# Weight stores queued behind later loads, more pieces kept from the first block, and one branch around two loops

## The chip, the cores and the metric

The kernel runs on one core of a Trainium2 chip. The core has five engines that run their own instruction streams: TensorE (PE, matrix products, with its weight loads as PEld), VectorE (DVE), ScalarE (ACT), GpSimd (POOL) and SyncE (SP), which here issues almost all DMAs. The streams wait for each other by semaphores. A DMA is issued by one instruction and runs on the core's 16 DMA engines. The metric is the device time of one execution in microseconds (us), the median of several.

## The reference

One decoder block of width 1024 over 2048 tokens, in float32. Cut to its steps:

```
h  = rmsnorm(x, g1);  p = h @ w_in            # q, k, v, r, gate ranks, u, two gates
a  = chunked gated linear attention(q, k, v)  # then per-head norm, times silu(r)
b  = multi-scale causal pooling(u)            # four windows, a map per group
x1 = x + (sig(gg) * (a @ w_a) + sig(gp) * (b @ w_b)) @ w_out
h2 = rmsnorm(x1, g2)
group = top 1 of 4 by softmax(h2 @ w_rg);  2 of the 8 experts of that group
y  = x1 + sum over the two experts of weight * SwiGLU(h2)
out = rmsnorm(y, gf)
```

Each of the 32 experts has a hidden width of 256.

## The kernel before

The tokens are handled in four blocks of 512. For each block `block` projects the inputs, runs the attention in chunks and the pooling branch, forms the gates and merges the two branches (`merge`, products on L757), multiplies by the output weights (`out_mm`, L774), adds the input, normalizes (`out_norm` calls `normed`), turns the result with transposing DMAs (`turn`, L261), and computes the router's logits (`logits`, L796). A block's logits are computed among the products of the next block. After the four blocks come 16 pairs of experts: up and gate products on L1297, down products on L1322 and L1334, the last norm in `finish`, and a scattered store of rows on L1284. At the end `overflow` has two loops that run only if an expert got more rows than its fixed capacity: the first redoes the surplus tiles, the second the last norm. Here both run zero times.

Most products are done in three passes of half-precision parts, so each weight piece (128×1024 float32, 512 KB) has to be split into a high and a low half. `stage` loads the piece (DMA on L161), `halves` converts it (ScalarE L177 for the high half, VectorE L178 for the low one), and the two halves are stored once to a scratch tensor in memory, `wkeep` (DMA on L181), from which later blocks load them with one DMA of the same size (L170). `KEEP` gives for each kind of weight the block from which on its pieces are stored; a piece not stored yet is loaded raw and converted again in the next block. The kinds are, in order: q, k and u; v and r; the two gates; the output weights (8 pieces); the attention branch (4 pieces); the pool branch, which is first folded with the pooling map (L725). Raw and converted pieces share one ring of `NW` = 13 buffers named `w`.

All these loads, stores and the transposing DMAs are issued by SyncE in one order. A DMA whose data isn't ready makes SyncE stand, and what is behind it stands too. The order on each engine is laid down when the program is built, by a scheduler which follows the code's order and the readiness of operands; `issue_after` ties an instruction's place to another's.

Of the kernel before, what the change touches and what calls it, by code (L numbers as in the profile page):

```python
# [16 lines left out]
D = 1024  # L17
KT = 8
# [18 lines left out]
class Mixer:  # L37
# [10 lines left out]
    def pools(self):  # L48
# [14 lines left out]

        self.C, self.kept = tc.dram_tile([16 + 40 + 24, 128, 2, 1024], F16, name="wkeep"), {}
# [24 lines left out]
    def consts2(self):  # L89
# [22 lines left out]
        self.g2q = self.cx.tile([128, D], F32, name="g2q")  # L112
        V.tensor_scalar(self.g2q, self.g2, float(D) ** 0.5, None, op0=OP.mult)
# [45 lines left out]
    def stage(self, mat, i):  # L159
        f = self.wp.tile([128, 1024], F32, name="w", bufs=self.NW)  # L160
        self.nc.sync.dma_start(f, self.A[mat][i])  # L161
        return f

    def weight(self, mat, i, f=None, c=0):

        nc = self.nc
        if (mat, i) not in self.kept:
            return self.halves(f or self.stage(mat, i), (mat, i))
        w = self.wp.tile([128, 2, 1024], F16, name="w", bufs=self.NW)
        nc.sync.dma_start(w[:, :, c:], self.C[self.kept[mat, i]][:, :, c:])  # L170
        return w

    def halves(self, f, key, c=0):
# [19 lines left out]
    KEEP = (1, 1, 0, 1, 1, 0)  # L193
# [10 lines left out]
    NW, NET, NBT = 13, 19, 13  # L204
# [11 lines left out]
    def normed(self, x, g, store=None, quick=False, new=None):  # L216

        nc = self.nc
        if quick:
# [11 lines left out]
            for y, n in zip(ys, q):  # L231
                nc.vector.scalar_tensor_tensor(y, x[:, n], r[:, 0:1], self.g2q[:, n], op0=OP.mult, op1=OP.mult)
# [569 lines left out]
    def block(self, b, tail):  # L802

        last = b + 1 == self.NB
        self.blk = b
        self.hT, self.L7, self.L7c = self.hTn, self.sevens(self.Hn, self.HSn), self.sevens_c(self.Hn, self.HSn)
# [56 lines left out]
        if last:  # L863
            self.xo = {t: self.x_load(b, t) for t in range(TT)}
# [206 lines left out]
    def spill(self):  # L1071
# [31 lines left out]
        V.tensor_scalar(none[:, 0:1], none[:, 0:1], 0.5, None, op0=OP.is_lt)  # L1103
        for _, _, l, _ in self.tab:
# [26 lines left out]
    def moe(self):  # L1131
# [18 lines left out]
        with tc.manual_schedule(engines={getattr(E, e) for e in self.MANUAL}) if self.MANUAL else ExitStack():  # L1150
            for P in range(self.NP + 1):
                for c in (self.PLAN if P else self.PLAN.replace("U0 A0 U1 A1", "V0 V1 W0 A0 W1 A1")).split():
# [186 lines left out]
    def finish(self, s, i):  # L1339

        nc = self.nc
        x, o, _, l, nl = s["X"][i]
        y, r = self.rstd(x)
# [7 lines left out]
        nc.vector.tensor_tensor(y, x, y, op=OP.mult)  # L1351
        t = self.scatter(y, o).ins
# [21 lines left out]
    def overflow(self):  # L1374
# [7 lines left out]
        with tc.For_i(0, n):  # L1382
            T = lambda name, sh, dt=F32: mp.tile([128] + sh, dt, name="o" + name)
            le = T("le", [32])
            V.tensor_scalar(le, self.ct, self.it, None, op0=OP.is_le)
            e = T("e", [1])
            V.tensor_reduce(e, le, axis=AX.X, op=OP.add)
            ei = T("ei", [1], I32)
            V.tensor_copy(ei, e)
            V.tensor_scalar(le, self.i32, e, None, op0=OP.is_equal)  # L1390
            st = T("st", [32])
            V.tensor_tensor(st, self.ct, self.nt, op=OP.subtract)
            V.tensor_tensor(st, st, le, op=OP.mult)
            base = T("base", [1])
            V.tensor_reduce(base, st, axis=AX.X, op=OP.add)
            V.tensor_tensor(base, self.it, base, op=OP.subtract)
            V.tensor_tensor(st, self.capE, le, op=OP.mult)
            cap = T("capt", [1])
            V.tensor_reduce(cap, st, axis=AX.X, op=OP.add)
            V.scalar_tensor_tensor(base, base, 128.0, cap, op0=OP.mult, op1=OP.add)  # L1400
            rel, oth = T("rel", [nt * 2]), T("oth", [nt * 2])
            V.tensor_scalar(oth, self.ex.rearrange("p t k -> p (t k)"), e, OOB, op0=OP.not_equal, op1=OP.mult)
            V.tensor_scalar(rel, self.rk.rearrange("p t k -> p (t k)"), base, None, op0=OP.subtract)
            V.tensor_tensor(rel, rel, oth, op=OP.add)
            io = T("io", [128])
            nc.gpsimd.iota(io, pattern=[[1, 128]], base=0, channel_multiplier=0, allow_small_or_imprecise_dtypes=True)
            pt = self.aux()
            for c in range(2 * nt):
                a = mp.tile([128, 128], F32, name="oA", bufs=1)
                V.tensor_scalar(a, io, rel[:, c:c + 1], None, op0=OP.is_equal)  # L1410
                nc.tensor.matmul(pt[:, 0:2], a, self.fld[:, c // 2, c % 2], start=c == 0, stop=c == 2 * nt - 1)
            tb = T("tb", [2, 1])
            V.tensor_copy(tb, pt[:, 0:2, None])
            ii, w, _, _ = self.columns(tb, "o", mp)
            er = nc.values_load(ei[0:1, 0:1], engines=[mybir.EngineType.SP], min_val=0, max_val=NE - 1,
                                skip_runtime_bounds_check_because="a count of at most 31")
            W = [[self.load(self.A["we"][bass.ds(er, 1), :, c:c + PW].rearrange("o p c -> p (o c)"), i == 2)
                  for c in range(i * 2048, (i + 1) * 2048, PW)] for i in range(3)]
# [114 lines left out]
```

## Time and profile before

| | |
|---|---|
| runs of the kernel, us | 1673.47, 1674.84, 1676.40 (median 1674.84) |
| profiled execution, us | 1676.06, its span 1674.3 |
| mean granted TensorE clock | 0.960 |
| busy in the span, us | PE 1530.3 (91%), DVE 1074.3 (64%), ACT 686.0 (41%), POOL 607.7 (36%) |
| moved by DMA | 294.03 MB read from memory, 75.50 MB written |

The span is the time from the first to the last instruction of the profiled execution, and all positions in it are us from its start. Block 0 ends, and block 1's projections begin, at about 340 us; block 1's gates follow at 497 us, the blocks' ends at about 630, 900 and 1150, and the experts run from about 1170 to 1653. A row of a timeline shows when an instruction (or a run of like ones, xN) started and how long it took; for TensorE the bracket tells the idle time before it and what ended that. SPq is SyncE's issuing of a DMA: its time includes waiting, not the transfer. The granted clock is a share of the full TensorE clock: 1.0 is 2.4 GHz, 0.5 is 1.2 GHz.

### The profile page before, as it was taken

The numbers are of one execution on the slowest core, as the hardware profiler recorded it, in microseconds if no ns is written. First come the engines' busy times: TensorE is split into PE (matmuls) and PEld (weight loads), VectorE is DVE, ScalarE is ACT, GpSimd is POOL, SyncE is SP. The second block draws the span as 40 slices with busy tenths as digits, with TensorE's granted clock in tenths as the row PEclk, the third lists the DMA queues.
The fourth block names the chain that finished last, engine by engine and source line by source line (L and its number), as shares of the span: only waits on it lengthen the run. The fifth ranks groups of instructions, "written<-read, shape, count | busy, mean of one in ns | idle before, by whom it ended". The sixth has DMA issues, their size and how long they took to land.

```text
span 1674.3 us, 27694 instructions
## 1 busy us (share of the span) xinstructions
PE 1530.3 (91%) x10587; PEld 914.6 (55%) x10587; DVE 1074.3 (64%) x1898; ACT 686.0 (41%) x1056; POOL 607.7 (36%) x543
## 2 busy tenths in 40 slices
PE   5898978987999898999989999996799999999994
PEld 3364333435744343764434674443668787777773
DVE  8669685589954543772624674337577777777762
ACT  5623453453223352122423021113356665666661
POOL 1356382356523401342322241121343444444431
PEclk9999999989999999999989999998799999999997
DMA  7434659797775989565878756759599999999941
GB/s 267 133 117 141 232 189 249 230 293 234 231 259 164 250 287 286 182 194 179 231 192 246 245 160 201 204 159 315 187 313 332 336 328 341 333 325 326 330 164 43
DMA packets 244808, 394.65 MB, mean 236 GB/s; under 512 B 154507, under 2 KB 157963, under 8 KB 244672
## 3 DMA queue, kind: packets, MB, share of 16 engines
q1 hardware_dynamic: 222144, 324.50, 62.5%
q0 software_dynamic: 22528, 68.35, 11.5%
q8 instruction: 84, 1.38, 0.3%
q14 instruction: 52, 0.43, 0.1%
HBM read 294.03 MB, written 75.50 MB: 221 GB/s over the span
## 4 chain that ended last, share of the span: by engine, by line
PE 66%; DVE 11%; DMA 7%; issue 6%; POOL 4%; SPq 3%; ACT 2%; POOLq 0%; DVEq 0%; ACTq 0%
PE acc L1297 14%; PE aux L339 8%; PE acc L774 8%; PE acc L339 8%; PE acc L1322 7%; PE acc L522 6%; PE acc L757 6%; DMA w<-in_wv_dram 4%; PE acc L1334 3%; DVE w L178 3%; DMA bt<-bt 2%; SPq L261 2%; PE auxh L1241 2%; PE acc L591 1%; POOL w L398 1%
## 5 line engine op out<-in xcount | busy, mean ns | idle before, releaser
L1297 PE MATMUL acc<-xT,mwh 128*128 128x184 f16 (+2 forms) x3264 | 249.8, 239 | 0.0
L1297 PEld LDWEIGHTS <-mwh 128*128 128x128 f16 x3264 | 244.6, 98 | 7.6 <-issue 7.6
L178 DVE SCALAR_TENSOR_TENSOR w<-w 128x1024 f16<-128x1024 f32 x106 | 144.2, 1369 | 88.5 <-ACT w L177 88.2
L774 PE MATMUL acc<-w,bt 128*128 128x512 f16 x768 | 174.4, 389 | 16.1 <-DMA bt<-bt 12.9
L339 PEld LDWEIGHTS <-hS 128*128 128x128 f16 x1056 | 104.5, 100 | 133.4 <-issue 18.0
L757 PE MATMUL acc<-w,bt 128*128 128x512 f16 x768 | 169.0, 381 | 7.1 <-ACT w L177 7.1
L177 ACT ACTIVATE w<-w 128x1024 f16<-128x1024 f32 x106 | 108.0, 1028 | 151.8 <-DMA w<-in_wv_dram 75.2
L1203 DVE SCALAR_TENSOR_TENSOR mwh<-mst,mwh 128x1024 f16<-128x1024 f32 x128 | 153.4, 1219 | 23.6 <-ACT mwh L1202 23.4
L1202 ACT ACTIVATE mwh<-mst 128x1024 f16<-128x1024 f32 x128 | 128.7, 1049 | 60.7 <-PE acc L1297 59.8
L774 PEld LDWEIGHTS <-bt 128*128 128x128 f16 x768 | 76.0, 100 | 113.2 <-issue 14.5
L339 PE MATMUL aux<-w,hS 128*128 128x512 f16 x528 | 131.6, 398 | 4.5 <-DVE w L178 2.5
L339 PEld LDWEIGHTS <-hT 128*128 128x128 f16 x792 | 77.2, 98 | 100.9 <-issue 11.1
L522 PEld LDWEIGHTS <-w 128*128 128x128 f16 x1176 | 114.3, 100 | 32.4 <-issue 10.5
L757 PEld LDWEIGHTS <-bt 128*128 128x128 f16 x768 | 75.3, 98 | 99.9 <-issue 10.9
L339 PE MATMUL acc<-w,hS 128*128 128x512 f16 x528 | 123.1, 382 | 0.0
L1322 PE MATMUL acc<-msd,sg 128*128 128x512 f32 x256 | 115.7, 605 | 0.0
L762 POOL TENSOR_TENSOR et<-et 128x512 f32<-128x512 f32 x32 | 40.5, 1269 | 174.9 <-DVE et L760 174.9
L684 ACT ACTIVATE bt<-et 128x512 f16<-128x512 f32 x48 | 30.2, 628 | 174.4 <-POOL et L762 100.6
L348 DVE SCALAR_TENSOR_TENSOR et<-aux,et 128x512 f32<-128x512 f32 x99 | 65.8, 683 | 53.5 <-PE aux L339 53.5
L339 PE MATMUL aux<-w,hT 128*128 128x512 f16 x396 | 91.8, 379 | 5.7 <-DVE w L178 3.3
L760 DVE SCALAR_TENSOR_TENSOR et<-acc,et 128x512 f32<-128x512 f32 x64 | 43.3, 689 | 82.4 <-PE acc L757 82.4
L339 PE MATMUL acc<-w,hT 128*128 128x512 f16 x396 | 92.3, 379 | 0.9 <-DVE w L178 0.9
(293 smaller groups left out, 2493.8 us busy)
## 6 DMA issues: line engine op xcount, KB each, us to landing
w<-wkeep SPq DMA_DIRECT2D x172, 512.0 KB, 4.7
mst<-in_we_dram SPq DMA_DIRECT2D x128, 512.0 KB, 6.0
wkeep<-w SPq DMA_DIRECT2D x70, 512.0 KB, 3.3
msd<-in_we_dram SPq DMA_DIRECT2D x64, 512.0 KB, 7.1
w<-in_wv_dram SPq DMA_DIRECT2D x60, 512.0 KB, 4.9
x<-in_x_dram SPq DMA_DIRECT2D x32, 512.0 KB, 5.5
w<-in_wm_dram SPq DMA_DIRECT2D x16, 512.0 KB, 6.1
out_dram<-x POOLq DMA_DIRECT2D x16, 512.0 KB, 5.8
```

What stands on the lines that cost most here:

```text
L177: nc.scalar.activation(w[:, 0, c:], f[:, c:], AF.Copy, scale=WSC)
L178: nc.vector.scalar_tensor_tensor(w[:, 1, c:], f[:, c:], WSC, w[:, 0, c:], op0=OP.mult, op1=OP.subtract)
L339: nc.tensor.matmul(p, L[name](i, c, k), w[k // 2][:, a, (k % 2) * 512:(k % 2 + 1) * 512], start=k == 0 and m == 0, stop=k == 3 and m == 2)
L348: nc.vector.scalar_tensor_tensor(o[i], ps[i], DSC, x[i], op0=OP.mult, op1=OP.add)
L522: nc.tensor.matmul(ps[:, :h], w[:, i, k * 128:(k + 1) * 128], L[name](c, k), start=k == 0 and m == 0, stop=k == 3 and m == 2)
L757: nc.tensor.matmul(ps, lhs, w[k // 2][:, a, (k % 2) * 512:(k % 2 + 1) * 512], start=k == 0 and i == 0, stop=k == 3 and i == 2)
L774: nc.tensor.matmul(ps, self.mT[t][k // 4][:, 4 * c + k % 4], w[hf][k // 2][:, a, (k % 2) * 512:(k % 2 + 1) * 512], start=k == 0 and i == 0 ...
L1202: nc.scalar.activation(w[:, 0], f, AF.Copy, scale=WSC)
L1203: nc.vector.scalar_tensor_tensor(w[:, 1], f, WSC, w[:, 0], op0=OP.mult, op1=OP.subtract)
L1297: nc.tensor.matmul(ps[:, c * CAP + lo:c * CAP + hi], self.part(W[o], col, 128, a), xT[:, b, k, lo:hi], start=k == 0 and i == 0, stop=k == ...
L1322: nc.tensor.matmul(ps, s["ac"][i][:, f, :128], self.part(s["W"][3 * i + 2], f * D + hf * 512, 512), start=f == 0, stop=f == 1)
L1334: nc.tensor.matmul(ps[hf * 64:(hf + 1) * 64], s["ac"][h][:, f, CAP - 64:], self.part(s["W"][3 * h + 2], f * D + hf * 512, 512), start=q == ...
```

## The change

1. A store of a converted piece is no longer issued where the piece is converted. It is put into a list, and issued right after the second load of a weight piece that follows (`AHEAD` = 2). What is left in the list is issued at the start of the next block.
2. `KEEP` stores the output weights and the attention branch from block 0 on instead of block 1 (12 pieces; 44 stores are now in block 0 instead of 32, and 30 in block 1 instead of 42). In block 1 these pieces are loaded converted, and their 12 conversions there go.
3. The ring of weight buffers has 14 instead of 13. The tile `g2q` goes; before the last block's end, `g2` is scaled in place on VectorE instead.
4. The last norm of the last two pairs of experts is computed in another way: squares on ScalarE in two halves, the gain premultiplied once in a tile `gl`, and one VectorE step per tile in place of one on ScalarE and one on VectorE. The last pair does its mixed tile ("2") first, then its two full tiles.
5. The two loops at the end stand in one branch on the first count.

```diff
     def stage(self, mat, i):
         f = self.wp.tile([128, 1024], F32, name="w", bufs=self.NW)
-        self.nc.sync.dma_start(f, self.A[mat][i])
+        self.loaded(self.nc.sync.dma_start(f, self.A[mat][i]).ins)
         return f
+    AHEAD = 2
+    def loaded(self, ins):
+        self.nload += 1
+        while self.stores and self.stores[0][0] + self.AHEAD <= self.nload:
+            with self.tc.issue_after(ins):
+                self.store1()
+    def store1(self):
+        _, n, w, c = self.stores.pop(0)
+        getattr(self.nc, self.KQ).dma_start(self.C[n][:, :, c:], w[:, :, c:])
+    def flush(self):
+        while self.stores:
+            self.store1()
...
-        nc.sync.dma_start(w[:, :, c:], self.C[self.kept[mat, i]][:, :, c:])
+        self.loaded(nc.sync.dma_start(w[:, :, c:], self.C[self.kept[mat, i]][:, :, c:]).ins)
...
             n = self.kept[key] = len(self.kept)
-            getattr(nc, self.KQ).dma_start(self.C[n][:, :, c:], w[:, :, c:])
+            self.stores.append((self.nload, n, w, c))
...
-    KEEP = (1, 1, 0, 1, 1, 0)
+    KEEP = (1, 1, 0, 0, 0, 0)
...
-    NW, NET, NBT = 13, 19, 13
+    NW, NET, NBT = 14, 19, 13
...
-                nc.vector.scalar_tensor_tensor(y, x[:, n], r[:, 0:1], self.g2q[:, n], op0=OP.mult, op1=OP.mult)
+                nc.vector.scalar_tensor_tensor(y, x[:, n], r[:, 0:1], g[:, n], op0=OP.mult, op1=OP.mult)
...
+            nc.vector.tensor_scalar(self.g2, self.g2, float(D) ** 0.5, None, op0=OP.mult)
...
+        self.gl = mp.tile([128, D], F32, name="gl")
+        nc.scalar.activation(self.gl, self.gf, AF.Identity, bias=self.lq[:, 1:2], scale=self.ln[:, 0:1])
...
+                if P == self.NP - 1:
+                    plan = plan.replace("D0 F0 D1 F1 D2 F2", "D2 F2 D0 F0 D1 F1")
...
+        if s["P"] >= 14:
...
+                for h in range(2):
+                    c = slice(h * 512, h * 512 + 512)
+                    nc.scalar.activation(y[:, c], x[:, c], AF.Square, accum_out=ss[:, h:h + 1])
+                nc.vector.tensor_scalar(r, ss[:, 0:1], ss[:, 1:2], D * EPS, op0=OP.add, op1=OP.add)
+                nc.gpsimd.tensor_tensor(r, r, self.mhalf[:, 0:1], op=OP.pow)
+                nc.vector.tensor_scalar(r, r, self.lq[:, 0:1], self.lq[:, 1:2], op0=OP.mult, op1=OP.add)
+                nc.vector.scalar_tensor_tensor(y, x, r, self.gl, op0=OP.mult, op1=OP.mult)
...
-        with tc.For_i(0, n):
+        with tc.If(n > 0):
+            with tc.For_i(0, n):
...
-        n = nc.values_load(self.tot[0:1, 1:2], min_val=0, max_val=nt, skip_runtime_bounds_check_because="0 or all tiles")
-        with tc.For_i(0, n) as t:
+            n = nc.values_load(self.tot[0:1, 1:2], min_val=0, max_val=nt, skip_runtime_bounds_check_because="0 or all tiles")
+            with tc.For_i(0, n) as t:
```

What moves on the engines is seen best in SyncE's order. First, block 0 before the merge, where the pool branch is folded. Before, L161 is a raw load and L181 a store; w_2124 and w_2133 are the raw pieces for the fold, hS and hT the next block's transposed input:

```order
L161 DMA w_2020<-in_wv_dram 128x1024
L161 DMA w_2022<-in_wv_dram 128x1024
L181 DMA wkeep_79<-w_1963 128x2048
L181 DMA wkeep_79<-w_1967 128x2048
L181 DMA wkeep_79<-w_2024 128x2048
L181 DMA wkeep_79<-w_2028 128x2048
L161 DMA w_2124<-in_wv_dram 128x1024
L161 DMA w_2133<-in_wv_dram 128x1024
L181 DMA wkeep_79<-w_2076 128x2048
L261 DMA_TRANSPOSE hS_2115<-et_2036 128x8x128
L181 DMA wkeep_79<-w_2080 128x2048
L261 DMA_TRANSPOSE hS_2115<-et_2037 128x8x128
```

The same place now; a raw load is L160, a store L174, a transposing DMA L277, and the fold's pieces are w_2120 and w_2129:

```order
L160 DMA w_2014<-in_wv_dram 128x1024
L160 DMA w_2016<-in_wv_dram 128x1024
L174 DMA wkeep_79<-w_1870 128x2048
L174 DMA wkeep_79<-w_1873 128x2048
L174 DMA wkeep_79<-w_1910 128x2048
L174 DMA wkeep_79<-w_1913 128x2048
L174 DMA wkeep_79<-w_1959 128x2048
L174 DMA wkeep_79<-w_1962 128x2048
L160 DMA w_2120<-in_wv_dram 128x1024
L160 DMA w_2129<-in_wv_dram 128x1024
L174 DMA wkeep_79<-w_2024 128x2048
L174 DMA wkeep_79<-w_2027 128x2048
```

The fold's two loads stood behind the stores of all four pieces before them. Now two of these stores are behind the loads, with stores of older pieces ahead.

Second, the end of block 0. Before, bt_2649 and bt_2650 are the first normed rows turned for the router, x is the next input, w_2831 and w_2833 are weights of block 1:

```order
L161 DMA w_2831<-in_wv_dram 128x1024
L181 DMA wkeep_79<-w_2793 128x2048
L181 DMA wkeep_79<-w_2797 128x2048
L161 DMA w_2833<-in_wv_dram 128x1024
L275 DMA x_4541<-in_x_dram 128x1024
L181 DMA wkeep_79<-w_2837 128x2048
L181 DMA wkeep_79<-w_2841 128x2048
L181 DMA wkeep_79<-w_2906 128x2048
L261 DMA_TRANSPOSE bt_2649<-bt_2575 128x8x128
L261 DMA_TRANSPOSE bt_2650<-bt_2576 128x8x128
L181 DMA wkeep_79<-w_2910 128x2048
L275 DMA x_4586<-in_x_dram 128x1024
```

The same place now, where the turned rows are bt_2657 and bt_2658:

```order
L174 DMA wkeep_79<-w_2759 128x2048
L174 DMA wkeep_79<-w_2762 128x2048
L160 DMA w_2839<-in_wv_dram 128x1024
L160 DMA w_2841<-in_wv_dram 128x1024
L174 DMA wkeep_79<-w_2803 128x2048
L174 DMA wkeep_79<-w_2806 128x2048
L291 DMA x_4543<-in_x_dram 128x1024
L277 DMA_TRANSPOSE bt_2657<-bt_2583 128x8x128
L277 DMA_TRANSPOSE bt_2658<-bt_2584 128x8x128
L291 DMA x_4588<-in_x_dram 128x1024
L160 DMA w_3052<-in_wv_dram 128x1024
L160 DMA w_3054<-in_wv_dram 128x1024
```

The three stores (w_2837, w_2841 and w_2906 before) have gone from in front of the two transposes to behind them.

Third, the end of the program on GpSimd. Before, y are finished tiles, L1371 the power of the last norm, L1380 and L1438 the loads of the two counts:

```order
L1371 TENSOR_TENSOR frs_17108<-frs_17108,mhalf_85 128x1
L1371 TENSOR_TENSOR frs_17130<-frs_17130,mhalf_85 128x1
L1284 DMA out_0_dram<-y_17109,tim_10488 2048x1024
L1284 DMA out_0_dram<-y_17131,tih_10521 4096x512
L1380 TENSOR_LOAD stot_10620
L1382 COMPARE_AND_BRANCH
L1382 ISA
L1382 UNCONDITIONAL_BRANCH
```

...and behind the first loop's body:

```order
L1382 REGISTER_ALU
L1382 COMPARE_AND_BRANCH
L1382 UNCONDITIONAL_BRANCH
L1438 TENSOR_LOAD stot_10620
L1439 COMPARE_AND_BRANCH
L1439 UNCONDITIONAL_BRANCH x2
```

Now, where L1436 is the load of the first count, L1438 the branch and L1439 the first loop:

```order
L1427 TENSOR_TENSOR frs_17059<-frs_17059,mhalf_85 128x1
L1386 TENSOR_TENSOR frs_17082<-frs_17082,mhalf_85 128x1
L1315 DMA out_0_dram<-y_17060,tih_10484 4096x512
L1386 TENSOR_TENSOR frs_17102<-frs_17102,mhalf_85 128x1
L1315 DMA out_0_dram<-y_17083,tim_10451 2048x1024
L1315 DMA out_0_dram<-y_17103,tim_10451 2048x1024
L1436 TENSOR_LOAD stot_10583
L1438 COMPARE_AND_BRANCH
L1439 COMPARE_AND_BRANCH
```

The mixed tile (tih) is scattered first now, and the last scatter is a full tile's. When the count is zero, L1438 skips both loops, with the load of the second count between them.

## Rows read from the trace of the kernel before

**Rows 1.** Windows: PE, PEld, DVE, ACT, POOL busy; granted clock, DMA share, GB/s.

```profile
246.70:250.00 3.30, 3.26 (x4) 1.32 (x5) 3.30 (x3) 1.13 (x2) 3.14 (x3) 0.51 0.17 68
...
357.00:365.00 8.00, 8.00 (x40) 3.29 (x37) 5.78 (x9) 3.05 (x4) 1.12 (x2) 0.65 1.02 395
365.00:395.00 30.00, 25.39 (x192) 13.81 (x190) 24.45 (x31) 11.66 (x16) 20.14 (x14) 0.89 1.08 309
395.00:430.00 35.00, 24.01 (x182) 18.57 (x179) 34.28 (x73) 8.27 (x13) 21.55 (x16) 0.90 0.41 142
1210.00:1650.00 440.00, 437.07 (x4066) 329.17 (x4066) 321.47 (x525) 269.56 (x357) 175.36 (x173) 0.99 0.86 302
```

**Rows 2.** SyncE's waits: waited-for instruction, us in total, times, longest.

```profile
SPq L181 <- DVE w L178: 115.2, 39, 9.2
```

**Rows 3.** SyncE's timeline, 229 to 244: start, us, engine, line, DMA, count.

```profile
229.61 12.53 SPq L181 DMA_DIRECT2D wkeep<-w  x4
242.24 1.21 SPq L161 DMA_DIRECT2D w<-in_wv_dram  x2
```

**Rows 4.** TensorE's timeline, 246 to 282; idle time before in brackets.

```profile
246.74 3.55 PE L725 MATMUL aux<-w,pwt 128*128 128x512 f32 x4 [3.00 <-DMA w<-in_wv_dram]
...
253.99 1.88 PE L725 MATMUL aux<-w,pwt 128*128 128x512 f32 x4
...
274.32 6.77 PE L757 MATMUL acc<-w,bt 128*128 128x512 f16 x24 [6.36 <-ACT w L177]
```

**Rows 5.** SyncE's timeline, 343 to 353.

```profile
343.69 4.69 SPq L181 DMA_DIRECT2D wkeep<-w  x3
348.48 4.39 SPq L261 DMA_TRANSPOSE bt<-bt  x2
```

**Rows 6.** TensorE's timeline, 341 to 371.

```profile
341.73 2.75 PE L339 MATMUL aux<-w,hS 128*128 128x512 f16 x12
...
354.29 0.19 PE L796 MATMUL aux<-wrh,bt 128*128 128x36 f16 x1 [2.47 <-DMA bt<-bt]
...
356.62 0.24 PE L796 MATMUL aux<-wrh,bt 128*128 128x36 f16 x2 [1.67 <-DMA bt<-bt]
...
357.29 4.43 PE L339 MATMUL aux<-w,hS 128*128 128x512 f16 x10
361.52 3.71 PE L339 MATMUL acc<-w,hS 128*128 128x512 f16 x14
...
370.69 0.21 PE L796 MATMUL aux<-wrh,bt 128*128 128x36 f16 x1 [3.73 <-DMA bt<-bt]
```

**Rows 7.** TensorE's timeline, first delayed router product of blocks 1 and 2.

```profile
642.83 0.24 PE L796 MATMUL aux<-wrh,bt 128*128 128x36 f16 x2 [4.75 <-DMA bt<-bt]
...
910.79 0.22 PE L796 MATMUL aux<-wrh,bt 128*128 128x36 f16 x2 [1.98 <-DMA bt<-bt]
```

**Rows 8.** The page's parts 5 and 6: conversions of weights, and their stores.

```profile
L178 DVE SCALAR_TENSOR_TENSOR w<-w 128x1024 f16<-128x1024 f32 x106 | 144.2, 1369 | 88.5 <-ACT w L177 88.2
...
L177 ACT ACTIVATE w<-w 128x1024 f16<-128x1024 f32 x106 | 108.0, 1028 | 151.8 <-DMA w<-in_wv_dram 75.2
...
wkeep<-w SPq DMA_DIRECT2D x70, 512.0 KB, 3.3
```

**Rows 9.** Timeline of all engines after the last product.

```profile
1652.95 0.75 DVE L1337 SCALAR_TENSOR_TENSOR mx<-acc,twr,mx 128x512 f32<-128x512 f32 x1 [0.99 <-PE acc L1334]
...
1659.68 0.99 POOL L1284 DMA_INDIRECT out_dram<-y,tih  x1 [1.48 <-DVE y L1351]
```

**Rows 10.** Lines L1382, L1438, L1439, L1529 on GpSimd: ns min/median/max, first and last start.

```profile
L1382 POOLq INC_SWDGE_SEM  x1: 1832/1832/1832, 1661.2 to 1661.2; - x1
...
L1438 POOLq TENSOR_LOAD <-stot x1: 306/306/306, 1664.7 to 1664.7; - x1
...
L1439 POOLq COMPARE_BRANCH  x3: 33/33/39, 1665.2 to 1666.5; - x3
...
L1529 POOLq DRAIN  x3: 40/109/6772, 1666.7 to 1674.0; - x3
```

More of the change, by code (lines that the diff above doesn't have):

```diff
@@ L62, in pools @@
         self.H = tc.dram_tile([self.NTOK, 2, D], F16, name="h2d")
+        self.stores, self.nload = [], 0
         self.C, self.kept = tc.dram_tile([16 + 40 + 24, 128, 2, 1024], F16, name="wkeep"), {}
@@ L1103, in spill @@
         V.tensor_scalar(none[:, 0:1], none[:, 0:1], 0.5, None, op0=OP.is_lt)
+        self.ln, self.lq = T("ln", [1]), T("lq", [2])
+        V.tensor_copy(self.ln, none[:, 0:1])
+        V.tensor_scalar(self.lq[:, 0:1], none[:, 0:1], float(D) ** 0.5, None, op0=OP.mult)
+        V.tensor_scalar(self.lq[:, 1:2], none[:, 0:1], -1.0, 1.0, op0=OP.mult, op1=OP.add)
+        self.gl = mp.tile([128, D], F32, name="gl")
+        nc.scalar.activation(self.gl, self.gf, AF.Identity, bias=self.lq[:, 1:2], scale=self.ln[:, 0:1])
         for _, _, l, _ in self.tab:
@@ L1339, in finish @@
     def finish(self, s, i):
-        nc = self.nc
+        nc, mp = self.nc, self.mp
         x, o, _, l, nl = s["X"][i]
+        if s["P"] >= 14:
+            n = x.shape[1]
+            if n == D:
+                ss = mp.tile([128, 2], F32, name="fs2", bufs=2)
+                r = mp.tile([128, 1], F32, name="frs", bufs=3)
+                y = mp.tile([128, D], F32, name="y", bufs=3)
+                for h in range(2):
[5 more added lines that the diff above has]
+                nc.vector.scalar_tensor_tensor(y, x, r, self.gl, op0=OP.mult, op1=OP.mult)
+            else:
+                y, r = self.rstd(x)
+                nc.vector.tensor_scalar(r, r, self.ln[:, 0:1], self.lq[:, 1:2], op0=OP.mult, op1=OP.add)
+                for h in range(2):
+                    p = slice(h * 64, h * 64 + 64)
+                    nc.vector.scalar_tensor_tensor(y[p], x[p], r[p], self.gl[p, h * 512:(h + 1) * 512], op0=OP.mult, op1=OP.mult)
+            return self.put(s, i, y, o)
         y, r = self.rstd(x)
@@ L1381, in overflow @@
                            skip_runtime_bounds_check_because="counts of the rows bound it")
-        with tc.For_i(0, n):
[L1383 to L1418, printed above, removed]
-            W = [[self.msplit(f, self.mw) for f in w] if i < 2 else w for i, w in enumerate(W)]
-            x = self.mxs[0]
-            o = self.out, ii
-            self.base1(x, o, True)
-            h = self.mhs[0]
-            self.gather(h, ii, True)
-            xT = mp.tile([128, 2, 2, KT, CAP], F16, name="xT", bufs=2)
-            for a in range(2):
-                pt = self.auxh()
-                for k in range(KT):
-                    nc.tensor.transpose(pt[:, k * 128:(k + 1) * 128], h[:, a * D + k * 128:a * D + (k + 1) * 128], self.identh)
-                self.evac(a, xT[:, 0, a, :, 0:128], pt.rearrange("p (k t) -> p k t", k=KT))
-            V.memset(xT[:, 0, :, :, 128:], 0.0)
-            s = {"W": W, "xT": xT, "ac": {}, "ps": {}}
-            self.mo_up(s, 0)
-            self.mo_act(s, 0)
-            self.mo_out(s, 0, x, w)
-            self.scatter(x, o)
-            V.tensor_scalar(self.it, self.it, 1.0, None, op0=OP.add)
```

78 lines of the change are left out of this document (69 added, 9 removed).

## The prediction

> **What bounds the kernel now.** I read the page's first part, then the table of windows, then TensorE's timeline for its idle stretches, and beside each of them SyncE's timeline, since SyncE issues every load, store and transposing DMA. The reader is to see that TensorE is the bound, but not evenly. In the expert stage it is busy for 437.07 of 440 us [rows 1], so nothing that only touches that stage's loads or conversions can pay. In the mixer blocks it waits in short gaps, most of them in block 0 (up to about 430 us), where weights are converted and SyncE stands for 115.2 us in front of stores whose conversion isn't done [rows 2]. Whatever stands behind such a store in SyncE's order waits with it. The last place is the end of the program, after the last product: about 21 us without TensorE [rows 9].
>
> The profiled execution took 1676.06 us (span 1674.3), 1.2 us above the median of 1674.84. Each gain and cost below is taken from 1676.06.
>
> **The change, part by part.**
>
> *Stores behind two more loads, at the fold (A).* At 229.61 SyncE begins four stores and is not through them for 12.53 us; only then, at 242.24, come the two loads of raw pieces for the pool branch's fold [rows 3]. TensorE waits 3.00 us for them at 246.74, and comes out at the lower of its two clock levels, 1.2 GHz (granted clock 0.51 from 246.7 to 250 [rows 1]): four products of L725 take 3.55 us, against 1.88 us for the same four at 253.99 [rows 4]. In the new order two of the four stores come after these loads, and the two that stay ahead belong to pieces loaded earlier. So the loads can start some microseconds sooner, and need only 3.00. I take the whole gap and the clock: −3.0 − (3.55 − 1.88) = −4.7. If the loads find no free buffer it is 0. The next gap, 6.36 us at 274.32 [rows 4], waits for a conversion whose load stands behind transposes, and these in the new order stand behind the same stores as before. I leave it: 0, from −2 to +2.
>
> *The first transposes of the normed rows (B).* At 343.69 three stores hold SyncE for 4.69 us, and the two transposes that the first router product needs follow at 348.48 [rows 5]. TensorE waits for them 2.47 and 1.67 us at 354.29 and 356.62; the 24 products after that take 4.43 + 3.71 = 8.14 us [rows 6]. Twelve such products take 2.75 us at 341.73 [rows 6], so 24 would take 5.50, and 2.64 us are lost to the clock (0.65 granted from 357 to 365 [rows 1]). The three stores now come behind the transposes. I take both gaps and half of the clock's loss, since the gap of 3.73 us at 370.69 [rows 6] remains and can drop the clock too: −4.14 − 1.3 = −5.4, bounds −6.8 and 0.
>
> *VectorE's stretch (C).* From 395 to 430 VectorE is busy for 34.28 of 35 us and TensorE for 24.01 [rows 1]. Removing queue waits can't shorten VectorE's work, only move it to an earlier, less full stretch (24.45 of 30 us just before). I take −2, of bounds −5 and 0.
>
> *Twelve more stores in block 0, and the order of the loads there (D).* Eight pieces of the output weights and four of the attention branch are now stored in block 0: 12 stores of 512 KB. They add no engine work there, as these pieces are converted in block 0 anyway. But between 365 and 395 the DMA engines' share is 1.08 at 309 GB/s [rows 1]; at that rate one store's data is 0.524 MB / 309 GB/s = 1.7 us, and 12 are 20 us. Also, the eight pieces behind the first output weights (four more output pieces, then the first of the next block) were loaded without a store between them; now stores, each behind a conversion, stand among them. The lower bound is 0 (the stores' data fits between 395 and 430, where the share is 0.41), the upper one 20. I take +5, about three stores' worth: spread evenly over the 130 us from 300 to 430, 12 × 30 / 130 = 2.8 of them fall into the 30 us where the share is above 1.
>
> *Block 1 without the twelve conversions (E).* Twelve conversions leave block 1: 12 × 1.37 us on VectorE, 12 × 1.03 us on ScalarE [rows 8], and 12 stores. TensorE isn't waiting for them directly, but waits for transposes that share the DMA engines with the stores: 4.75 us at 642.83, while the same wait in block 2, which has no stores, is 1.98 us at 910.79 [rows 7]. −2.8, bounds −7 and 0.
>
> *One branch around both loops (F).* On GpSimd the first loop's skip holds a wait of 1.83 us for its queue that ends at 1663.0; then follow its exit, the second load of a count at 1664.7 (0.31 us), the second loop's branches from 1665.2 to 1666.5, and the drain of 6.77 us from 1666.7 [rows 10]. With one branch the second load, skip and exit go (1664.7 to 1666.7, 2.0 us), and part of the 1.7 us between 1663.0 and 1664.7. I take −3.0, bounds −3.7 and −1, as the drain may start from another event.
> The Trainium skill, "DMA: Bandwidth & Descriptors", section "Latency and other measured facts", gives a floor of about 600 ns to a tensor_load. The row shows 0.31 us, so the measurement decides; by the page's figure F would be −3.3.
>
> *The last experts' finish (G).* From the end of the last product to the last scatter it now takes 1659.68 − 1652.95 = 6.73 us [rows 9]. The new order ends with a full tile: on VectorE one half-row step (0.75 us, [rows 9]), two more of about that size, and two of 128×1024 at about 1.37 us (the nearest row of that form, [rows 8]): 3 × 0.75 + 2 × 1.37 = 5.0 us. The small steps and handovers between them have no row; with none of them G would be 5.0 − 6.7 = −1.7. I take a third of that, −0.6, bounds −2 and +2: the last scatter now writes twice the bytes.
>
> The scaling of the gain in place, the three small steps before the experts and the extra weight buffer: 0. ScalarE and VectorE have slack there, and a buffer only lets loads run further ahead.
>
> Sum: −4.7 − 5.4 − 2 + 5 − 2.8 − 3.0 − 0.6 = −13.5, so 1676.06 − 13.5 = 1662.6 us; against the median that is −12.2 us, or −0.7%.
>
> **The rivals.**
>
> *Only the end pays (R1).* The gaps of A and B only turn into waits for VectorE, which is 98% busy just behind them, so that C's stretch takes longer by what was won before; E brings nothing, as those transposes wait for merges on other engines. For it: VectorE's 34.28 of 35 us. Against: the 12.53 us in which loads stood behind stores. Left are F and G: 1676.06 − 3.6 = 1672.5.
>
> *More loads early, and block 0 keeps pace (R2).* The queue never stands in front of a store, conversions move up, and the 6.36 us at 274.32 and 3.73 us at 370.69 [rows 4, 6] go too, with C's 5: 1662.6 − 10.1 − 3 = 1649.5. Against: both wait behind work that the change doesn't move.
>
> *The stores push out what TensorE waits for (R3, slower).* The place is 300 to 430 us: with a DMA share of 1.08 the 20 us of added store data delay the transposes and the next block's loads that are queued behind them. A and B are then lost and the 20 us shown in full: 1676.06 − 2 − 2.8 − 3.6 + 20 = 1687.7. It is slower than before once more than 2 + 2.8 + 3.6 = 8.4 us of the 20 are exposed. Against: 395 to 430 has room.
> [...]
>
> *The change doesn't do what it says (R4).* The loads, which have only one more buffer, wait for it as long as they waited for the stores: A to D are 0, and E, F and G give 1676.06 − 6.4 = 1669.7.
>
> **How the numbers follow.** My forecast, with its own range of 1655 to 1669, has 0.52; R1 0.15; R2 0.10; R3 0.10; R4 0.13. The range of 8 in 10 leaves out most of R3 and the far end of R2: 1648 to 1676. What a measurement of this kernel can tell from no change is about 0.2%, or 3.4 us, so faster is below 1671.4 and slower above 1678.2. Faster: all of the forecast and R2, nearly all of R4 (0.11) and a third of R1 (0.05): 0.78. Within 0.2%: the rest of R1 and R4 and a third of R3's spread (it starts at 1668 with nothing exposed): 0.14. Slower: 0.08.
>
> **What would show it.** A: TensorE has no gap before the first fold products, and their loads leave SyncE before the last two stores. B: the two transposes leave before the three stores, and the first router product follows without 2.47 us of waiting. C: VectorE's dense stretch is shorter. D: the DMA share from 300 to 430 rises; wrong if TensorE gets a new gap that waits for a weight load. E: 94 conversions rather than 106, and a first router gap in block 1 near block 2's 1.98. F: one load of a count, then the drain, and about 11.6 us from the last scatter's issue to the end of the span (14.6 before). The forecast is wrong if block 0 ends no earlier than before, or if the gap at 274.32 grows by what the earlier ones lost.

## The result and the profile after

The changed kernel is slower: 1699.01 us (median of 4 runs, 1695.32 to 1699.79) against 1675.62 (1673.47 to 1679.93), a ratio of 1.0139 (95% interval 1.0116 to 1.0161). The forecast was 1662.6, with a range that ended at 1676. The profiled execution took 1699.79 us, span 1698.0.

To find where the time went I paired the products of TensorE by their place in its order, as their number is the same in both traces (10587), and took the difference of their starts. Between 351 and 400 the two kernels issue the router's small products at different places, so a single row there is good to a few us only:

| product, by its start in the kernel before | after minus before, us |
|---|---|
| block 0, second gate merge's end, 278 | +0.6 |
| first products of block 1, 340 | +3.8 |
| 351 | +14.9 |
| 414 | +18.6 |
| 433 | +22.7 |
| block 1, first merge, 508 | +22.1 |
| block 1, end of the output stage, 622 | +23.5 |
| behind block 1's delayed router products, 678 | +19.9 |
| block 3, 1141 | +20.3 |
| experts, 1205 (was +18.2 at 1191) | +25.5 |
| last instruction | +23.7 |

So most of it, 18.9 us, is lost between 340 and 433, and 3.2 us between 278 and 340. Behind block 1 the two traces differ by 3.6 us less at the router products, by 7.3 us more at the start of the experts and by about 2 us less at the end of the program. Other traces show the first two of these three steps in kernels whose code there is as before (see e1_tail, and E below), so I do not count them as the change's.

The windows at that place, columns as in [rows 1]: first two of the kernel before, then three of the changed kernel:

```profile
300.00:340.00 40.00, 39.94 (x179) 17.71 (x178) 27.20 (x29) 20.38 (x26) 13.83 (x11) 0.99 0.72 245
340.00:365.00 25.00, 20.86 (x105) 9.01 (x104) 22.73 (x25) 15.21 (x22) 11.58 (x10) 0.86 0.92 297
```

```profile
300.00:340.00 40.00, 37.61 (x171) 16.82 (x169) 22.08 (x23) 19.85 (x23) 7.78 (x6) 1.00 0.96 313
340.00:365.00 25.00, 17.41 (x71) 7.16 (x70) 22.11 (x20) 15.65 (x23) 11.14 (x10) 0.86 0.56 194
365.00:395.00 30.00, 21.82 (x114) 8.95 (x113) 25.61 (x27) 10.93 (x12) 17.23 (x13) 0.77 0.92 306
```

The reader is to see the second row of the changed kernel: where TensorE loses most (17.41 of 25 us busy) the DMA engines' share is down to 0.56, at 194 GB/s. TensorE does not wait there for a full DMA system. In the 40 us before, the DMA engines are fuller than they were (0.96 against 0.72), so whether the loads were late because they left late or because they took long has to be read from the loads themselves. SyncE's timeline of the changed kernel just before (L160 raw load, L174 store, L277 transposing DMA):

```profile
315.21 0.33 SPq L174 DMA_DIRECT2D wkeep<-w  x1
315.59 0.42 SPq L160 DMA_DIRECT2D w<-in_wv_dram  x1
318.99 0.33 SPq L174 DMA_DIRECT2D wkeep<-w  x1
319.41 0.38 SPq L160 DMA_DIRECT2D w<-in_wv_dram  x1
320.72 3.25 SPq L174 DMA_DIRECT2D wkeep<-w  x2
324.07 1.78 SPq L160 DMA_DIRECT2D w<-in_wv_dram  x2
326.29 0.33 SPq L174 DMA_DIRECT2D wkeep<-w  x1
326.71 1.42 SPq L160 DMA_DIRECT2D w<-in_wv_dram  x2
331.20 2.75 SPq L174 DMA_DIRECT2D wkeep<-w  x2
334.01 1.26 SPq L160 DMA_DIRECT2D w<-in_wv_dram  x2
```

Load and store take turns, and most stores wait for a conversion first. The kernel before issued eight of these loads in one go; its SyncE timeline has

```profile
302.61 12.21 SPq L161 DMA_DIRECT2D w<-in_wv_dram  x8
```

The last four of the eight are block 1's first v and r pieces; in the changed kernel these leave at 324.07 and 326.71, 12 us and more later. GpSimd, which subtracts such pieces first (L414), and then TensorE of the changed kernel show the effect:

```profile
333.88 2.36 POOL L414 TENSOR_TENSOR w<-w 128x1024 f32<-128x1024 f32 x1 [32.01 <-DMA w<-in_wv_dram]
```

```profile
348.12 2.75 PE L355 MATMUL acc<-w,hS 128*128 128x512 f16 x12
356.47 1.01 PE L355 MATMUL acc<-w,hS 128*128 128x512 f16 x2 [5.59 <-ACT w L193]
357.73 5.52 PE L355 MATMUL acc<-w,hS 128*128 128x512 f16 x18 [0.25 <-DVE w L194]
366.09 1.02 PE L355 MATMUL acc<-w,hS 128*128 128x512 f16 x4 [2.84 <-DVE w L194]
```

GpSimd stood for 32.01 us until a raw piece landed, and TensorE waits 5.59 and 2.84 us for conversions where before it ran on and waited for transposes only [rows 6]. That piece, by its semaphore the first of the pair issued from 326.71, took 7.2 us from leaving to use. The eight loads of the kernel before landed after

```profile
DMA to landing us min/median/max: 3.6/5.3/7.8
```

So the piece was late because its load left late, not because the load took longer.

### The profile page after: what moved, and what is told of

Read it like the earlier page. It is cut to its first block, busy times and chain, and to the rows that moved or that the text cites. A ratio compares the mean times of both kernels' runs of the same rounds, so it can differ in the third digit from the quotient of the medians.

```text
span 1698.0 us, 27511 instructions
## 1 busy us (share of the span) xinstructions
PE 1538.9 (91%) x10587; PEld 917.5 (54%) x10587; DVE 1077.9 (63%) x1891; ACT 674.1 (40%) x1047; POOL 606.7 (36%) x543
## 3 DMA queue, kind: packets, MB, share of 16 engines
q0 software_dynamic: 22528, 68.35, 11.4%
## 5 line engine op out<-in xcount | busy, mean ns | idle before, releaser
L790 PE MATMUL acc<-w,bt 128*128 128x512 f16 x768 | 174.8, 389 | 18.5 <-DMA bt<-bt 12.5
L1234 DVE SCALAR_TENSOR_TENSOR mwh<-mst,mwh 128x1024 f16<-128x1024 f32 x128 | 153.5, 1218 | 26.1 <-ACT mwh L1233 24.9
L193 ACT ACTIVATE w<-w 128x1024 f16<-128x1024 f32 x94 | 95.1, 1025 | 135.9 <-DMA w<-in_wv_dram 60.1
L355 PE MATMUL acc<-w,hT 128*128 128x512 f16 x396 | 95.9, 390 | 5.3 <-DVE w L194 4.6
```

Of the source, the lines that this page charges most:

```text
L193: nc.scalar.activation(w[:, 0, c:], f[:, c:], AF.Copy, scale=WSC)
L355: nc.tensor.matmul(p, L[name](i, c, k), w[k // 2][:, a, (k % 2) * 512:(k % 2 + 1) * 512], start=k == 0 and m == 0, stop=k == 3 and m == 2)
L790: nc.tensor.matmul(ps, self.mT[t][k // 4][:, 4 * c + k % 4], w[hf][k // 2][:, a, (k % 2) * 512:(k % 2 + 1) * 512], start=k == 0 and i == 0 ...
L1234: nc.vector.scalar_tensor_tensor(w[:, 1], f, WSC, w[:, 0], op0=OP.mult, op1=OP.subtract)
```

## The experiments

Two theories. **Order**: what counts is which DMA stands in front of which on SyncE; stores that wait for conversions, or that hold buffers, make loads late. **Data**: the 6.3 MB more in block 0 fill the DMA engines. Ratios are against the kernel before on the same chip. Its median was 1675.6 beside the changed kernel and 1675.7 for e1_tail to e4_o1, but 1669.6 to 1670.6 on the chips of the other runs, so from f1_keep_act on a total is also given as the microseconds that its ratio makes of that median, and this is held against the expectation.

**e1_tail**, the end alone (finish, order of the last pair, gain, branch): `KEEP`, `NW` and the stores as before.

> The kernel before with the parts at the end alone: the last pairs' finish and order, the gain scaled in place, and one branch around both loops; stores, KEEP and the 13 buffers as before. In the changed kernel the end of the program gave 3.2 us for the branch and cost 1.1 for the finish (the last scatter waits behind the mixed tile's), and about 5 us were lost at the start of the experts, where all engines stood. Theory 'code': this stall comes with the new code, so it is here too: 1675.6 + 5 - 2.1 = about 1678.5, with blocks 0 to 3 unchanged. Rival 'placement in time': the stall is an accident of which loads are in flight then, and isn't here: about 1673.5.

1673.67 against 1675.66, ratio 0.9990 (0.9976 to 1.0003): about the rival's number, and not clear of no change. But the stall at the start of the experts is in its profile: from TensorE's 6100th to its 6400th product 18.5 us, against 14.1 in the profile of before and 21.4 after. It is also in e2_keep (20.6) and e3_defer (20.9), which have the kernel before's code there, and it is not in e7_imm, f6_ahead4 and f7_halfO (13.4 to 13.6), which have the changed kernel's. So the new code there does not make it, and I do not count it as a cost of the change. The four traces of the chip of e1_tail to e4_o1 have it (18.5 to 20.9), and so has that of the changed kernel (21.4); the eleven others, with either code, lie at 13.4 to 15.2. Its cause stays open.

**e2_keep**, the kept pieces alone:

```diff
-    KEEP = (1, 1, 0, 1, 1, 0)
+    KEEP = (1, 1, 0, 0, 0, 0)
```

> The kernel before with KEEP = (1, 1, 0, 0, 0, 0) alone: 12 stores move to block 0, each issued where its piece is converted. Theory 'order' (SyncE stands in front of the new stores, so the loads of the next block's v and r pieces come after conversions): TensorE gets a gap of 5 to 15 us between 330 and 400 that waits for weight conversions, block 1's end gives 3 to 4 back, total 1683 to 1692. Rival 'data' (the 6.3 MB of added stores fill the DMA engines): the same loss spread over 300 to 430 with gaps that wait for landings, total near 1690. Rival 'deferral' (only the queueing behind two loads does harm): 1671 to 1674.

1695.98, ratio 1.0121 (1.0091 to 1.0150), above what the three theories gave. The kept pieces alone cost nearly as much as the whole change, but for the larger part elsewhere, at the fold. SyncE and TensorE there:

```profile
235.01 18.13 SPq L181 DMA_DIRECT2D wkeep<-w  x4
253.24 0.38 SPq L161 DMA_DIRECT2D w<-in_wv_dram  x1
257.24 0.32 SPq L181 DMA_DIRECT2D wkeep<-w  x1
259.45 5.34 SPq L261 DMA_TRANSPOSE hT<-et  x4
264.88 5.42 SPq L261 DMA_TRANSPOSE hS<-et  x4
270.36 0.57 SPq L161 DMA_DIRECT2D w<-in_wv_dram  x1
```

```profile
274.77 3.78 PE L725 MATMUL aux<-w,pwt 128*128 128x512 f32 x4 [13.64 <-DMA w<-in_wv_dram]
```

The fold's second load now leaves at 270.36, behind eight transposes: adding stores made the scheduler lay SyncE's order anew.

**e3_defer**, the deferral alone, in the kernel before:

```diff
-            getattr(nc, self.KQ).dma_start(self.C[n][:, :, c:], w[:, :, c:])
+            self.stores.append((self.nload, n, w, c))
```

> The kernel before with the stores queued behind the next two loads (AHEAD = 2) alone; KEEP and 13 buffers as before. Theory 'order': without stores among the output pieces' loads the v and r loads leave in a burst as before, near 302 us, and the time is within 5 us of the kernel before: 1671 to 1680. Rival 'deferral': the deferred stores hold buffers longer and stand in front of later loads; most of the loss is here, 1688 to 1698. Rival 'data': no more stores in block 0 than before, 1672 to 1676.

1696.69, ratio 1.0131 (1.0098 to 1.0164): the rival 'deferral' by the total. 'Order' is missed by 17 us. Here the loads do leave in a run at the end of block 0, but nine of them take 18.24 us, where before eight took 12.21:

```profile
307.35 18.24 SPq L162 DMA_DIRECT2D w<-in_wv_dram  x9
```

SyncE's waits in this run are for buffers: 10.6 us until a conversion has freed one, 3.1 us until a load has landed, and none for a store. So that a put-off store keeps its buffer is not what made this run long, as far as the trace shows; f6_ahead4 is where loads wait for stores to land (14.6 us in six waits before 455). What costs the 21 us here is not shown.

**e4_o1**, the changed kernel with the output weights kept from block 1 again (`KEEP = (1, 1, 0, 1, 0, 0)`):

> The changed kernel with the output weights stored from block 1 on again (KEEP = (1, 1, 0, 1, 0, 0)), so 4 stores are added to block 0 instead of 12; all else as changed. Theory 'order': no stores stand among the loads of the output and the next v and r pieces, the waits of 5.6, 2.8, 1.9 and 2.7 us between 351 and 386 go, 12 to 18 us less than the changed kernel: 1681 to 1687. Rival 'data': 8 of 12 stores go, two thirds of some 20 us: 1685 to 1689, with gaps left in proportion. Rival 'deferral': little changes, 1694 to 1700.

1696.7, ratio 1.0129 (1.0096 to 1.0161): the total is that of the rival 'deferral'. At the one place that 'order' named it holds: from the product at 340 to that at 378 it wins 2.6 us where the changed kernel loses 12.3. But 6.6 us go earlier (302 to 319, TensorE waiting 5.18 us for VectorE to empty a result) and 7.2 in block 1's output stage, so the total is not explained by it.

**f1_keep_act**, e2_keep with the stores in ScalarE's stream:

```diff
-    KQ = 'sync'
+    KQ = 'scalar'
```

> The kernel before with KEEP = (1, 1, 0, 0, 0, 0) and all stores issued by ScalarE (KQ = 'scalar') instead of SyncE: the same 44 stores in block 0 as in e2_keep, in another instruction stream. Theory 'order' (a load or transposing DMA is late because a store stands in front of it on SyncE): the 13.6 us in front of the fold's product go, the next v and r loads leave early, and the time falls well below e2_keep's 1696; 1665 to 1680, the upper end if ScalarE's standing in front of VectorE's halves delays its own conversions. Rival 'data' (the added bytes fill the DMA engines): the same bytes at the same time, 1690 to 1700.

1702.57, ratio 1.0192 (1.0167 to 1.0217), that is +32: by the total neither. The wait at the fold is gone, as 'order' says. The loss is now from 378 to 390 (14.5 us), where TensorE waits for router transposes. Their landings from 300 to 430, first in the kernel before and then here, with the window of that stretch here:

```profile
DMA to landing us min/median/max: 3.6/6.3/11.8
```

```profile
DMA to landing us min/median/max: 5.8/15.1/21.4
```

```profile
365.00:400.00 35.00, 20.29 (x112) 8.19 (x112) 22.60 (x25) 9.86 (x11) 12.12 (x10) 0.75 1.16 217
```

The transposing DMAs land at a median of 15.1 us instead of 6.3, with the DMA share at 1.16 but only 217 GB/s moved. Within this run the five issued from 366 to 395, with six stores of ScalarE's stream among them, take 14.3 to 21.4 us, and the two issued at 349 and 351 take 5.8. So 'data' has a part where stores meet transposes, which SyncE's single order mostly keeps apart. The Trainium skill, "DMA: Bandwidth & Descriptors", section "Queues, rings and completion order", says that a DMA engine takes turns between the queues that have work for it. The 15.1 us against 6.3 fit that; no row here shows the turns themselves.

**f3_keepO** and **f4_keepBG**, the two parts of e2_keep: the output weights alone (`KEEP = (1, 1, 0, 0, 1, 0)`) and the attention branch alone (`KEEP = (1, 1, 0, 1, 0, 0)`).

> The kernel before with the output weights alone stored from block 0 on (KEEP = (1, 1, 0, 0, 1, 0)), stores issued at once: 8 of e2_keep's 12 added stores. In SyncE's order the fold's two loads stand together as before (in e2_keep the second is laid behind eight transposes). Theory 'order': TensorE's wait at the fold stays near 3 us instead of 13.6; stores now stand among the loads of the last output pieces and of the next v and r pieces, so the gap that waits for weights near 350 is here (5 to 10 us); block 1's end gives 3 back: 1679 to 1686. Rival 'data': two thirds of e2_keep's 20 us, wherever: 1688 to 1691.

> The kernel before with the attention branch alone stored from block 0 on (KEEP = (1, 1, 0, 1, 0, 0)), stores issued at once: 4 of e2_keep's 12 stores. In SyncE's order the fold's second load goes behind eight transposes, as in e2_keep. Theory 'order': the wait at the fold's product is 12 to 14 us again, though only a third of the stores is added, and nothing is late at 350: +8 to +14 over the kernel before. Rival 'data': a third of e2_keep's +20, +6 to +7, without the long wait at the fold.

f3_keepO 1687.61, 1.0106 (1.0085 to 1.0126), that is +17.7; f4_keepBG 1682.86, 1.0076 (1.0046 to 1.0106), +12.7. By place both go as 'order' says: in f3_keepO the fold's wait is 2.76 us, and a wait of 2.87 us for a conversion appears at 352, shorter than the 5 to 10 foretold; in f4_keepBG the fold's wait is 13.60 us, with a third of the stores. By the total only f4_keepBG does: it fits 'order' (+8 to +14) and not 'data' (+6 to +7). f3_keepO's expectations were reckoned from 1675.7, +3 to +10 for 'order' and +12 to +15 for 'data'; +17.7 is above both, and nearer to 'data'.

**g1_bg_pre** settles what makes the fold late. It is f4_keepBG with the two raw loads traced earlier:

```diff
+            if b == 0:
+                self.fpre = {BP0 + 2 + j: self.stage("wv", BP0 + 2 + j) for j in range(2)}
             self.p0_turn(0, nx, self.DM[1])
```

> f4_keepBG with the fold's two raw loads of the second merge traced ahead of the next block's transposing DMAs: in SyncE's order the second load stands right behind the first again instead of behind eight transposes; the four added stores stay in their places. Theory 'order' (the place of that load makes the wait): TensorE's 13.6 us at the fold fall to 3 to 6 us, and the kernel is 6 to 10 us faster than f4_keepBG, +2 to +7 over the kernel before. Rival 'data' (the added stores make it late): the wait stays above 10 us, +10 to +14.

```profile
232.02 17.98 SPq L181 DMA_DIRECT2D wkeep<-w  x4
250.09 1.20 SPq L161 DMA_DIRECT2D w<-in_wv_dram  x2
```

With the same stores in front, both loads leave at 250.09 and the 13.6 us are gone altogether. But what the kernel gains isn't clear of the noise: 1681.85, ratio 1.0055 (1.0036 to 1.0074), against 1.0076 (1.0046 to 1.0106). At +9.2 the total lies between the two ranges. Other waits take its place: 4.07 us for the merge's weights, 3.09 for output weights, 4.55 and 3.75 for router transposes. The cause of the wait is shown; my price for it (6 to 10 us) was wrong.

**f7_halfO**, the changed kernel with only the second four output pieces kept from block 1, so that just the stores go that stand among block 1's first loads:

```diff
-            return 1 if i < GG0 else 2 if i < O0 else 3 if i < BG0 else 4 if i < BP0 else 5
+            return 1 if i < GG0 else 2 if i < O0 else (3 if i < O0 + 4 else 6) if i < BG0 else 4 if i < BP0 else 5
...
-    KEEP = (1, 1, 0, 0, 0, 0)
+    KEEP = (1, 1, 0, 0, 0, 0, 1)
```

> The changed kernel with the second four output pieces stored from block 1 on again: in SyncE's order only the four stores go that stand between their loads and those of the next block's first v and r pieces, and the first of these loads stand in one run of six. Theory 'order': the v and r conversions come earlier, TensorE's waits of 5.6 and 2.8 us at 351 and 363 go (as in e4_o1, which took away all eight), 8 to 14 us less than the changed kernel's +23 over the kernel before: +9 to +15. Rival 'data': 4 of 12 added stores, a third of the loss: +15 to +17, and the waits at 351 only shorter. Rival 'the output pieces are not it': +20 or more.

1682.73, ratio 1.0089 (1.0059 to 1.0118), that is +14.9 us, with an interval from +10 to +20: the total can't tell 'order' (+9 to +15) from 'data' (+15 to +17). The place can. TensorE there:

```profile
349.33 8.37 PE L355 MATMUL acc<-w,hS 128*128 128x512 f16 x38
```

The 38 products run through without the 5.59 and 2.84 us. SyncE stands for conversions as long as in the changed kernel (24.9 and 24.3 us from 296 to 345), but six loads now leave in a run from 315.59, ahead of most of that. The four stores that went hold 1.7 us of data each by the prediction's rate, 7 us; their place among the loads cost 11 us at this one spot. This run takes bytes and places away together; that the loads took no longer in the changed kernel is what speaks for the places.

**e7_imm** and **f6_ahead4**, the changed kernel with stores at once, and with `AHEAD = 4`:

> The changed kernel with each store issued at once again, all else as changed (KEEP, 14 buffers, the end). SyncE's order at the fold is that of e2_keep. Theory 'order': the 13.6 us wait at the fold returns, and the stores of output pieces stand among the next loads as in the changed kernel; with the end's 2 us: +16 to +22. Rival 'deferral is the main harm': +5 or less. Rival 'deferral helps, as the change supposes': well above the changed kernel, +28 or more.

> The changed kernel with AHEAD = 4: each store waits for four further loads. At the end of block 0 six loads of v and r pieces then stand in a run with one store among them. Theory 'order': SyncE stands less for conversions there, and the gap at 351 is below 5 us; but a buffer is held until its store has landed, so loads wait for buffers instead: +12 to +22. Rival 'data': unchanged, +20 to +25. If queueing behind more loads is what was missing: +5 or less.

e7_imm 1693.7, 1.0146 (1.0118 to 1.0175), with 13.68 us at the fold; f6_ahead4 1697.0, 1.0178 (1.0146 to 1.0211), with 10.09 us at 305 for an output piece's conversion. e7_imm is at 'order' (+24, a little above its range), f6_ahead4 above all ranges. So the deferral does what it says at the fold (no wait of 13.7 us there in the changed kernel) and gives it back elsewhere. Queueing further back is no better: with `AHEAD` = 2 the interval was 1.0116 to 1.0161.

**e8_nw14**, e1_tail with `NW` = 14:

> e1_tail with 14 instead of 13 weight buffers: no deferral, KEEP as before. Theory 'order', with a scheduler that lays SyncE's order anew for every edit: the time depends on what moves; with the loads only further ahead, 1668 to 1676. Rival 'any edit costs' (the order of before is the best of many and any new one loses some 15 to 20 us in block 0): 1688 to 1695. If a buffer helps as the change supposes, it is below e1_tail's 1673.7 by 2 us or more.

1677.91, ratio 1.0053 (1.0038 to 1.0067): +8.8, between the two theories. With a buffer more the kernel is slower by half a per cent than before, not faster; the order is laid anew with it too, so what the buffer alone does is not separated from that.

**e9_if**, the branch alone, and **g3_if_bg_pre**, g1_bg_pre with it:

```diff
-        with tc.For_i(0, n):
+        with tc.If(n > 0):
+            with tc.For_i(0, n):
```

> The kernel before with the one branch around both loops alone. In the changed kernel it gave 3.2 us (14.6 to 11.4 us from the last scatter to the end), while the finish cost 1.1. So 3 us below the kernel before: 1672.5, and about 1 us below e1_tail. Rival: the branch's gain is in the profile only, 1675 to 1676.

> g1_bg_pre with the one branch around both loops (4 us in e9_if). Theory 'order': +2 to +7 less 4, so -2 to +3 against the kernel before; it beats the branch alone (-4) only if the fold's wait falls below what it was before, since block 1's end gives 3 to 4 for the missing conversions. Rival 'data': +6 to +10.

e9_if 1666.3 against 1669.74, ratio 0.9976 (0.9964 to 0.9987): faster, and the best version. From the last scatter, here at 1653.85, to the end of the span at 1665.3 it takes 11.4 us, against 14.6. g3_if_bg_pre 1677.29, ratio 1.0039 (1.0024 to 1.0053), that is +6.5: above the 'order' range (−2 to +3) and at the low end of 'data' (+6 to +10). The gain hoped for in block 1 does not pay for block 0.

Taken together, 'order' names the places of the long waits, and g1_bg_pre and f7_halfO bear it out there. It does not give the totals: of the versions with moved stores, f4_keepBG is within its range, f7_halfO at the edge of it, e7_imm just above, and e2_keep, e3_defer, e4_o1, f1_keep_act, f3_keepO, g1_bg_pre, g3_if_bg_pre and f6_ahead4 are slower than it said.

## Why the prediction was wrong

**A, the fold's loads: the order right, the worth not.** SyncE and TensorE of the changed kernel, answering to [rows 3] and [rows 4]:

```profile
234.09 1.23 SPq L160 DMA_DIRECT2D w<-in_wv_dram  x2
236.06 17.58 SPq L174 DMA_DIRECT2D wkeep<-w  x4
256.87 4.00 SPq L277 DMA_TRANSPOSE hS<-et  x3
```

```profile
243.95 1.29 PE L355 MATMUL aux<-w,hT 128*128 128x512 f16 x4 [3.03 <-DVE w L194]
263.12 13.58 PE L773 MATMUL acc<-w,bt 128*128 128x512 f16 x50 [5.92 <-ACT w L193]
```

The loads leave 8.2 us earlier, and the wait of 3.00 us at the fold is gone; TensorE waits 3.03 us for VectorE instead. From the product at 232 to that at 278 it comes to +0.1, not −4.7. That is R1's mechanism. Nor was the whole gap there to win: in e9_if, with the order of before, it is 1.65 us, with 2.62 us for VectorE just behind. The stores still cost SyncE 17.58 us, now in front of the transposes.

**B: wrong.** The two transposes leave at 347.95, hardly earlier than before (348.48), as two other stores stand ahead of them:

```profile
341.57 5.07 SPq L174 DMA_DIRECT2D wkeep<-w  x2
...
347.95 4.91 SPq L277 DMA_TRANSPOSE bt<-bt  x2
```

That was in the order's rows, and I counted only the three that had gone.

**C: wrong.** From 395 to 430 VectorE is less dense (30.16 us against 34.28), but only since its work comes later: from 413 to 448 it is busy for 34.90 of 35 us, and −2 was not won.

```profile
395.00:430.00 35.00, 27.22 (x217) 18.82 (x218) 30.16 (x46) 10.56 (x16) 22.47 (x16) 0.90 0.73 233
```

**D is the step that failed.** I let the 12 stores cost DMA time, +5 us by their bytes, bounds 0 to 20, and passed over the loads that "were loaded without a store between them" in one sentence without a price. The price was there in the rows: 12.53 us for four stores [rows 3]. Measured, the end of block 0 and the start of block 1, from 340 to 433, lose 22.7 − 3.8 = 18.9 us. Of these 14.9 − 3.8 = 11.1 come at the two waits for conversions, 5.59 and 2.84 us, with slower products between them (18 in 5.52 us, where 12 take 2.75), and f7_halfO takes them away. Right behind, the kernel before has 4.14 us of router waits [rows 6] that the changed kernel hasn't, so part of the 11.1 is made good at once; the rest of the 18.9 are shorter waits up to 433, whose cause no run settles. So D's size was within its bounds, but it was an order of loads that cost it, not bytes. R3 named the place and the sign, but by a full DMA system, which the share of 0.56 and the 7.2 us of the late load contradict. With A, B and C at their bounds of 0 and D at 20, my own terms give 1689.7; the range should have reached there. The measured 1699.0 is 9 us more still, and 7.3 us of it stand at the start of the experts, where no term of mine was.

**E: the count right, the time by luck.** The conversions, answering to [rows 8], and the first two router waits of block 1, answering to [rows 7]:

```profile
L194 DVE SCALAR_TENSOR_TENSOR w<-w 128x1024 f16<-128x1024 f32 x94 | 143.7, 1537 | 62.1 <-ACT w L193 61.9
...
L193 ACT ACTIVATE w<-w 128x1024 f16<-128x1024 f32 x94 | 95.1, 1025 | 135.9 <-DMA w<-in_wv_dram 60.1
```

```profile
662.81 0.22 PE L812 MATMUL aux<-wrh,bt 128*128 128x36 f16 x2 [1.28 <-DMA bt<-bt]
673.38 0.19 PE L812 MATMUL aux<-wrh,bt 128*128 128x36 f16 x1 [3.59 <-DMA bt<-bt]
```

94 conversions as foretold, the wait of 4.75 is 1.28, and −3.6 us came against −2.8. But e9_if, whose stores and conversions in block 1 are those of before, has

```profile
640.64 0.22 PE L796 MATMUL aux<-wrh,bt 128*128 128x36 f16 x2 [1.95 <-DMA bt<-bt]
```

and −4.7 us from the product at 622 to that at 678; e1_tail has 2.39 us and −2.6. So the 4.75 us were long in the one trace of before, whatever the stores, and I priced E by them. That fewer stores in block 1 won anything is not shown.

**F: right,** −3.2 against −3.0. **G: wrong by its sign,** +1.0 for −0.6. The end of the changed kernel:

```profile
1678.86 0.74 DVE L1356 SCALAR_TENSOR_TENSOR mx<-acc,twm,mx 128x512 f32<-128x512 f32 x1
...
1681.80 1.76 POOL L1315 DMA_INDIRECT out_dram<-y,tih  x1 [2.64 <-ACTq L1438]
1683.59 0.58 POOL L1386 TENSOR_TENSOR frs<-frs,mhalf 128x1 f32<-128x1 f32 x1
1684.36 1.03 POOL L1315 DMA_INDIRECT out_dram<-y,tim  x1 [0.19 <-issue]
...
1686.58 0.98 POOL L1315 DMA_INDIRECT out_dram<-y,tim  x1 [1.19 <-DVE y L1388]
```

```profile
L1586 POOLq DRAIN  x3: 44/113/6770, 1690.4 to 1697.7; - x3
```

From the last product's step at 1678.86 to the last scatter it takes 7.7 us, against 6.7 [rows 9]: GpSimd issues the mixed tile's scatter for 1.76 us before it comes to the last tile's power at 1683.59. VectorE waits 1.56 us for that power. My sum went over VectorE and left out GpSimd's order. One load and one branch, then the drain: 11.4 us from the last scatter to the end, where I had said 11.6.

What stays open: kept pieces alone (+20 us), deferral alone (+21) and both (+23) don't add up. In g1_bg_pre a wait taken away in block 0 is in good part replaced by later ones; why the total stays near 20 is not shown.

## What to carry to other kernels

A DMA queue fed by one in-order engine is a schedule of its own: before moving a store, list what then stands behind it, and price that by the longest time the queue has stood for such a store, not by its bytes alone (here 12.53 us for four stores, whose data is 7 us). Where a scheduler lays the order, compare the whole order of the queue, since an edit in one place moves loads in others. Before a wait is priced from one trace, look at it in a second trace of code that is the same there: the 3.00 us of A and the 4.75 us of E were 1.65 and 1.95. Take the parts of a change one at a time: here the one that paid was the branch.

## What the runs showed of the hardware

Router transposes landed at a median of 15.1 us instead of 6.3 when weight stores ran beside them from a second engine's stream (f1_keep_act). Skipping one empty loop and the load of its count at the end of the program was worth 3.2 us by the profiles, 3.4 by the medians of e9_if and the kernel before. The start of the experts took 13.4 to 15.2 us in eleven traces and 18.5 to 21.4 in five, and the code there doesn't decide which; all four traces of one chip are among the five. The kernel before ran at medians of 1669.6 to 1670.6 us on three chips and 1675.7 on that one.
